# Selected and sliding attention heads wait for the copy of the compression's sums instead of the compressed keys

## The chip, the cores and the metric

The kernel runs on one core of one Trainium2 chip. The metric is the device time of one execution in microseconds (us); the median of the runs is compared. The engines are named as in the profile: PE (TensorE, matmuls), PEld (its weight loads), DVE (VectorE), ACT (ScalarE), POOL (GpSimd) and SP (SyncE, which issues most DMAs).

## The reference, cut to what matters

Two decoder layers on 256 rows of 1024 channels, all in float32. In each layer one projection of the normalised rows feeds three attentions, whose outputs are gated, lifted to 1024 channels, merged and projected again.

```python
def hybrid_layer(x, ...):
    h = rms_norm(x, norm_g)
    (mq, mk, mv, mz, nq, kc, vc, ksl, vsl, kw, vw, ng, nz,
     fq, fk, fv, ff, fz, gl) = split(h @ w_in)
    # A) MoBA, 6 heads: at 256 rows, plain causal attention with rope
    y_moba = (o_moba * silu(mz)) @ w_up_moba
    # B) NSA, 4 query heads over one key head, three branches:
    k_cmp = nsa_compress(kc, ...)      # blocks of 32 rows, every 16:
    v_cmp = nsa_compress(vc, ...)      #   silu((block + pe) @ w1) @ w2
    # o_c: softmax(q . k_cmp) v_cmp      compressed, 15 keys
    # o_s: softmax(q . ksl) vsl          selected (all 4 blocks, causal)
    # o_w: softmax(q . kw) vw            sliding (window 512, causal)
    o_nsa = gc[0] * o_c + gc[1] * o_s + gc[2] * o_w
    y_nsa = (o_nsa * silu(nz)) @ w_up_nsa
    # C) FoX, 6 heads: causal attention with a cumulated log forget gate
    y_fox = (o_fox * silu(fz)) @ w_up_fox
    merged = g[0] * y_moba + g[1] * y_nsa + g[2] * y_fox
    return x + merged @ w_out
```

Only o_c needs the compressed keys and values. o_s and o_w need q, ksl, vsl, kw, vw.

## The kernel before, in words

**Dense work.** Every weight is streamed from DRAM once, in tiles of up to 128 x 1024 values. For exactness each is split in two: ACT rounds the tile into its high part `wh` (L262), DVE subtracts that and keeps the remainder `wl` (L263). Each block of a product is then three matmuls (L287, L288, L289: `wh` with the high part of the activations, `wl` with it, `wh` with their remainder). They are called dense here; most have 384, 390 or 512 columns. Accumulators "acc" hold four banks of PSUM.

**Small work.** Heads and compression use PE between the dense matmuls. Tiles called "at" share a pool of three PSUM banks: which bank a new one takes is fixed when the kernel is built, and its first matmul waits until the last reader of the tile before it in that bank is done. They hold transposes of query and key columns (L475, for q: ACT copies half, L488, DVE takes the remainder, L489, and both again for the other half of the rows, twice for two tiles of rows), the sums' transpose and hidden layer of the compression (L804), the product with its second weight (L817), scores of a pair (L569, L582, L583, read by DVE's L589) and transposes of the exponentials (L596, read by L598 on ACT or L600 on DVE). One bank, "o", takes turns: first the sums U of the compression (L793, L794), then one group of head outputs after another (L604 to L608, L882).

**Compression.** `mm_w1` multiplies blocks by the first weight and leaves the sums U in bank "o". `cmp_post` copies them (L800), adds pairs of half blocks by a matmul (L804), applies the SiLU (L809 to L812), multiplies by the second weight (L817), normalises and rotates the key (L824 to L835), transposes it (L844) and lays it out for the four heads.

**What sets the order.** A planner lays out PE's whole list when the kernel is built. It holds a clock of planned time, which each dense step advances by 0.00042 us a column and matmul. `unit(generator, deps, lag)` puts a piece of small work on a list; it is due when its deps are done and the lag has passed, and each `yield` gives the planned time to its next part. `pairs` puts heads on the list two at a time. On PE this order is kept as written, so a small matmul that waits holds the dense ones behind it. The orders of DVE and ACT are made by a scheduler from the same program.

Dense blocks follow as in `run`: the NSA projections, `mq`, the first weight of the compression, `mz`, then `mk`, `fv`, `fq`, `fz`, `fk`, and the gate projections of 512 columns. `hs` are the selected and sliding heads, `hc` the compressed ones, `hm` MoBA's and `hf` FoX's; they take the bank "o" in this order of registration (`in_turn`).

Of the kernel before, what the change touches and what calls it, by code (L numbers as in the profile page):

```python
# [9 lines left out]
F32 = mybir.dt.float32  # L10
F32R = mybir.dt.float32r
AF = mybir.ActivationFunctionType
# [11 lines left out]
CL, CS, CH = 32, 16, 256  # L24
# [69 lines left out]
def trunk(ctx, tc, x, w_in, b_gate, cmp_w1, w_up_moba, w_up_nsa, w_up_fox, w_out, gains_d, eye_d, x_t, small_d, row_d, out):  # L94
    nc = tc.nc
    V, A, G, T = nc.vector, nc.scalar, nc.gpsimd, nc.tensor
# [90 lines left out]
    def unit(gen, deps=(), lag=1.5, limit=None):  # L187
        u = {"gen": gen, "deps": list(deps), "lag": lag, "limit": limit, "at": 0.0, "done": None}
        waiting.append(u)
        return u  # L190
# [159 lines left out]
    def layer(l):  # L350
        w = w_in[l]
        sh = {}
# [290 lines left out]
        def pairs(heads, deps):  # L643

            def both(hs):
                due = {}
                while len(due) < len(hs):
                    for i, h in enumerate(hs):
                        if i not in due:
                            lag = next(h)  # L650
                            if lag is not None:
                                due[i] = clock[0] + lag + i * SECOND
                while due:
                    i = min(due, key=due.get)
                    yield max(0.0, due[i] - clock[0])
                    try:
                        due[i] = clock[0] + next(hs[i])
                    except StopIteration:
                        del due[i]
            return [unit(both(heads[i:i + 2]), deps, LAG_K, HEADS) for i in range(0, len(heads), 2)]  # L660
# [33 lines left out]
        def nsa_heads(g):  # L694

            joints = [{} for _ in range(2)]

            def head(i, bank, rsum):
                h, b = 2 * g + i // 2, i % 2
                return attend(sh["nqs"][:, h, :], [sh[n][:, b, :] for n in ("kh2", "kl2")],  # L700
                              lambda kt: sh[("vsl", "vw")[b]][:, kt, :], i, bank, i, rsum, joint=joints[i // 2])
            return group(4, head, lambda bank, rsum: gated(bank, rsum, g))
# [81 lines left out]
        def mm_w1(b, ps):  # L784
# [3 lines left out]
            for q in range(8):  # L788
# [6 lines left out]
                if q % 4 == 3:  # L795
                    tick(8 * 0.11)

        def cmp_post():
            Us = wk.tile([64, CH], F32, name="zf", bufs=1)
            A.activation(Us[0:63], sh["U"][0:63, 0:CH], AF.Copy)  # L800
            yield 1.8
            ps = pat.tile([128, 512], F32, name="at")
            for c in range(2):
                T.matmul(ps[:, c * 32:c * 32 + 30], Us[0:63, c * 128:(c + 1) * 128],  # L804
                         tabs[0:63, K_SEL:K_SEL + 30], start=True, stop=True)
            hid = ps[:, 0:64].rearrange("p (c j) -> p c j", c=2)[:, :, 0:30]
            sg = sm.tile([128, 2, 30], F32, name="sg")
            hs = sm.tile([128, 2, 30], F32, name="hs")
            A.activation(sg, hid, AF.Exp, scale=-1.0)  # L809
            V.tensor_scalar(sg, sg, 1.0, None, op0=ALU.add)  # L810
            V.reciprocal(sg, sg)
            V.tensor_tensor(hs, hid, sg, op=ALU.mult)  # L812
            yield LAG_C
            ps = pat.tile([128, 512], F32, name="at")
            for kv in range(2):
                for c in range(2):
                    T.matmul(ps[0:NCMP, kv * HD:(kv + 1) * HD], hs[:, c, kv * NCMP:(kv + 1) * NCMP],  # L817
                             w2s[:, l, kv, c, :], start=c == 0, stop=c == 1)
            kc = sm.tile([16, 2, HD], F32, name="kc", bufs=1)[0:NCMP]
            vc = sm.tile([16, HD], F32, name="vc", bufs=1)[0:NCMP]  # L820
            ssc = sm.tile([16, 1], F32, name="ssc")[0:NCMP]
            rsc = sm.tile([16, 1], F32, name="rsc")[0:NCMP]
            jk = sm.tile([16, HD], F32, name="jk", bufs=1)[0:NCMP]
            A.activation(vc, ps[0:NCMP, HD:2 * HD], AF.Copy)  # L824
            A.activation(jk, ps[0:NCMP, 0:HD], AF.Square, accum_out=ssc)
            rsqrt(rsc, ssc, 1.0 / HD, (NCMP, 1))
            V.tensor_scalar(kc, ps[0:NCMP, 0:HD][:, None, :].to_broadcast([NCMP, 2, HD]), rsc, None, op0=ALU.mult)
            V.tensor_tensor(kc, kc, ncg[0:NCMP, l, :][:, None, :].to_broadcast([NCMP, 2, HD]), op=ALU.mult)
            ra = sm.tile([16, 2, 16], F32, name="ra")[0:NCMP]
            rb = sm.tile([16, 2, 16], F32, name="rb")[0:NCMP]  # L830
            cr = tabs[0:NCMP, K_CROPE:K_CROPE + 32]
            G.tensor_tensor(ra, kc[:, :, 0:16], cr[:, None, 0:16].to_broadcast([NCMP, 2, 16]), op=ALU.mult)
            G.tensor_tensor(rb[:, :, 0:8], kc[:, :, 8:16], cr[:, None, 16:24].to_broadcast([NCMP, 2, 8]), op=ALU.mult)
            G.tensor_tensor(rb[:, :, 8:16], kc[:, :, 0:8], cr[:, None, 24:32].to_broadcast([NCMP, 2, 8]), op=ALU.mult)
            G.tensor_tensor(kc[:, :, 0:16], ra, rb, op=ALU.add)  # L835
            kcb = lay.tile([128, 2, 32], F32, name="kcb")
            vcb = lay.tile([128, 4, HD], F32, name="vcb")
            G.memset(kcb, 0.0)
            G.memset(vcb, 0.0)
            for h in range(4):  # L840
                A.activation(vcb[32 * h:32 * h + NCMP, h, :], vc, AF.Copy)
            yield 7.0
            ps = pat.tile([128, 512], F32, name="at")
            T.transpose(ps[:, 0:NCMP], kc.rearrange("p a d -> p (a d)"), ident[0:NCMP, 0:NCMP])  # L844
            for a in range(2):
                V.tensor_copy(kcb[a * 64:a * 64 + 64, a, 0:NCMP], ps[a * 64:a * 64 + 64, 0:NCMP])
            sh["kcb"], sh["vcb"] = kcb, vcb
# [251 lines left out]
        def run(starts, following):  # L1099
            mm_first(starts)  # L1100
            if l == 0:
                mm("mv0")
                start_r()
                late_consts()
                rope_tables()
                ua = unit(post_a())
            else:
                start_r()
                rope_tables()
                ua = unit(post_a())  # L1110
                mm("mv0")
            cmp_zeros()
            uz = unit(cmp_tokens())
            mm("mv1")
            uv = unit(v_post("mv"))
            if l == 0:
                zero_lows()
                later_loads()
            mm("b0")
            finish(uz)  # L1120
            mm("w0")
            mm("b1")
            ub = unit(post_b())
            mm("mq0")
            mm("w1")
            mm("mq1")
            uq = unit(qk_post("mq"))
            mm("w2")
            mm("mz0")
            mm("mz1")  # L1130
            unit(z_post())
            mm("w3")
            uc = unit(cmp_post())
            hs = pairs(nsa_heads(0) + nsa_heads(1), [ua, ub, uc])
            hc = unit(cmp_heads(), [uc, ua], 1.5, HEADS)
            mm("mk0")
            mm("mk1")
            uk = unit(qk_post("mk"))
            hm = pairs(heads3("mq", "mk", "mv", 0, 0, False) + heads3("mq", "mk", "mv", 1, 0, False), [uq, uk, uv])
            mm("fv0")  # L1140
            mm("fv1")
            uv = unit(v_post("fv"))
            mm("fq0")
            mm("fq1")
            uq = unit(qk_post("fq"))
            mm("fz0")
            mm("fz1")
            uf = unit(fz_post())
            mm("fk0")
            mm("fk1")  # L1150
            uk = unit(qk_post("fk"))
            hf = pairs(heads3("fq", "fk", "fv", 0, 640, True) + heads3("fq", "fk", "fv", 1, 640, True),
                       [uq, uk, uv, uf])
            every = hs + [hc] + hm + hf
            for c in range(5):
                mm_gl(c, sh["gls"][c])
            finish(*every)
            g0, g1 = unit(gate_out(0)), unit(gate_out(1))
            unit(gate_sig(0))
            unit(gate_sig(1))  # L1160
            mm_gl(5, sh["gls"][5])
            unit(gate_sig(2))
            mm_up(0, sh["ups"][0], {0: [g0], 1: [g1]})
            m0 = unit(merged_T(0))
            mm_up(1, sh["ups"][1], {})
            m1 = unit(merged_T(1))
            finish(m0)
            state["sigs"] = sigs
            mm_out(sh["outs"], following)
            finish(m1)  # L1170
# [38 lines left out]
```

## Time and profile before

| what | value |
|---|---|
| median of 3 runs | 513.24 us (512.78 to 515.78) |
| profiled execution | 513.7 us, span 511.9 us |
| mean granted clock of PE | 0.997 |
| PE, PEld | busy 500.2 and 447.0 us |
| DVE, ACT, POOL | busy 399.9, 334.7 and 63.9 us |
| DMA | 92.31 MB, mean 180 GB/s |

The span runs from the first to the last instruction. A busy time is the time in which the engine had at least one instruction in flight; matmuls overlap, so the time from one start to the next is the price of a dense matmul, not its duration. A row of the timeline has the start, the duration, and in brackets the idle time before it with the instruction that ended it.

### The profile page before, as it was taken

The numbers are of one execution on the slowest core, as the hardware profiler recorded it, in microseconds if no ns is written. First come the engines' busy times: TensorE is split into PE (matmuls) and PEld (weight loads), VectorE is DVE, ScalarE is ACT, GpSimd is POOL, SyncE is SP. The second block draws the span as 40 slices with busy tenths as digits, with TensorE's granted clock in tenths as the row PEclk, the third lists the DMA queues.
The fourth block names the chain that finished last, engine by engine and source line by source line (L and its number), as shares of the span: only waits on it lengthen the run. The fifth ranks groups of instructions, "written<-read, shape, count | busy, mean of one in ns | idle before, by whom it ended". The sixth has DMA issues, their size and how long they took to land.

```text
span 511.9 us, 8226 instructions
## 1 busy us (share of the span) xinstructions
PE 500.2 (98%) x2806; PEld 447.0 (87%) x2806; DVE 399.9 (78%) x846; ACT 334.7 (65%) x645; POOL 63.9 (12%) x88
## 2 busy tenths in 40 slices
PE   9959999999999999999999999999999999999997
PEld 7859999999888888888889999999988888888886
DVE  6587988689986656998586998778997854698953
ACT  6677767877586675554376987678766866655440
POOL 3420121010020004024200000000101000142300
PEclk9998999999999999999999999999999999999999
DMA  8999885465665334655547699556547443537502
GB/s 288 323 224 239 218 270 162 131 217 165 190 203 183 121 93 160 193 178 180 170 124 189 185 242 278 184 154 194 180 157 242 144 148 101 165 125 229 178 5 82
DMA packets 58802, 92.31 MB, mean 180 GB/s; under 512 B 3964, under 2 KB 33288, under 8 KB 58760
## 3 DMA queue, kind: packets, MB, share of 16 engines
q1 hardware_dynamic: 56736, 89.67, 58.4%
q10 hardware_dynamic: 2024, 2.12, 1.3%
q8 instruction: 22, 0.36, 0.3%
q14 instruction: 20, 0.16, 0.1%
HBM read 90.71 MB, written 1.06 MB: 179 GB/s over the span
## 4 chain that ended last, share of the span: by engine, by line
PE 89%; ACT 5%; DVE 4%; issue 1%; ACTq 0%; DVEq 0%
PE acc L287 24%; PE acc L288 23%; PE acc L289 23%; PE at L596 2%; PE acc L1085 2%; ACT wh L262 2%; DVE wl L263 2%; PE at L582 1%; PE at L336 1%; PE at L583 1%; PE o L604 1%; PE o L608 1%; PE o L606 1%; PE o L794 1%; PE at L475 1%; PE o L793 1%
## 5 line engine op out<-in xcount | busy, mean ns | idle before, releaser
L263 DVE TENSOR_TENSOR wl<-st,wh 128x1024 fp32r<-128x1024 f32 (+4 forms) x180 | 200.6, 1122 | 51.3 <-ACT wh L262 49.8
L262 ACT ACTIVATE wh<-st 128x1024 fp32r<-128x1024 f32 (+4 forms) x180 | 170.6, 953 | 98.4 <-PE acc L289 71.9
L287 PE MATMUL acc<-wh,hT 128*128 128x512 f32 (+4 forms) x560 | 217.2, 388 | 1.8 <-ACT v L442 1.8
L288 PE MATMUL acc<-wl,hT 128*128 128x512 f32 (+4 forms) x560 | 203.0, 363 | 0.2 <-DVE wl L263 0.2
L289 PE MATMUL acc<-wh,lT 128*128 128x512 f32 (+4 forms) x560 | 203.2, 363 | 0.0
L289 PEld LDWEIGHTS acc<-wh,lT 128*128 128x128 f32 x560 | 105.4, 188 | 11.0
L287 PEld LDWEIGHTS acc<-wh,hT 128*128 128x128 f32 x560 | 106.1, 189 | 9.3 <-ACT v L442 2.1
L288 PEld LDWEIGHTS acc<-wl,hT 128*128 128x128 f32 x560 | 106.1, 190 | 7.2 <-DVE wl L263 0.7
L591 ACT ACTIVATE p<-p,nm 128x128 f32<-128x128 f32 x80 | 35.5, 445 | 17.4 <-DVE nm L589 17.2
L967 POOL TENSOR_TENSOR z<-z,tmp 128x512 f32<-128x512 f32 x8 | 12.9, 1649 | 108.3 <-ACT tmp L964 108.3
L287 PE MATMUL acc<-wh,qkT 128*128 128x512 f32 x64 | 25.6, 400 | 0.0
L289 PE MATMUL acc<-wh,qkT 128*128 128x512 f32 x64 | 25.0, 391 | 0.0
L288 PE MATMUL acc<-wl,qkT 128*128 128x512 f32 x64 | 25.0, 390 | 0.0
L1005 POOL TENSOR_TENSOR mg<-mg,tmp 128x512 f32<-128x512 f32 x8 | 15.8, 1996 | 51.5 <-DVE tmp L1004 51.5
L596 PE MATMUL at<-ident,p 128*128 128x128 f32 x120 | 19.8, 273 | 1.0 <-ACT qkT L496 1.0
L794 PE MATMUL o<-wl,Z 128*63 128x256 f32 x64 | 16.0, 287 | 3.3 <-DVE wl L263 3.3
L589 DVE CUSTOM_DVE_ANT_0 p<-at,tabs 128x128 f32<-128x128 f32 (+1 forms) x56 | 16.8, 349 | 2.7 <-ACT qkT L498 2.7
L953 DVE SCALAR_TENSOR_TENSOR gl<-acc,rt,tmp 128x512 f32<-128x512 f32 x24 | 17.0, 742 | 1.4 <-PE o L608 1.1
L596 PEld LDWEIGHTS at<-ident,p 128*128 128x128 f32 x120 | 15.0, 147 | 3.4 <-issue 1.6
L598 ACT ACTIVATE pt<-at 128x384 f32<-128x384 f32 x20 | 9.7, 487 | 9.8 <-PE at L596 9.4
L446 ACT ACTIVATE sq<-acc,rt 128x384 f32<-128x384 f32 (+2 forms) x28 | 13.7, 488 | 3.7 <-PE acc L289 3.2
L793 PE MATMUL o<-wh,Z 128*63 128x256 f32 x64 | 15.8, 285 | 0.1
(242 smaller groups left out, 685.6 us busy)
## 6 DMA issues: line engine op xcount, KB each, us to landing
st<-in_w_in_dram SPq DMA_DIRECT2D x52, 512.0 KB, 3.5
st<-in_w_in_dram SPq DMA_DIRECT2D x56, 384.0 KB, 4.3
st<-in_cmp_w_dram SPq DMA_DIRECT2D x32, 256.0 KB, 4.5
st<-in_w_out_dram SPq DMA_DIRECT2D x16, 512.0 KB, 4.3
st<-in_w_in_dram SPq DMA_DIRECT2D x8, 396.0 KB, 5.3
st<-in_w_in_dram SPq DMA_DIRECT2D x8, 390.0 KB, 3.1
tmp<-in_b_gate_dram SPq DMA_DIRECT2D x12, 256.0 KB, 3.7
st<-in_w_up_moba_dram SPq DMA_DIRECT2D x4, 512.0 KB, 3.6
```

Source lines behind the costliest of these rows:

```text
L262: return (lambda: A.activation(h, s_, AF.Copy), lambda: V.tensor_tensor(lo, s_, h.bitcast(F32), op=ALU.subtract))
L263: lambda: V.tensor_tensor(lo, s_, h.bitcast(F32), op=ALU.subtract))
L287: T.matmul(ps, sh, wh, start=first, stop=False)
L288: T.matmul(ps, sh, wl, start=False, stop=False)
L289: T.matmul(ps, sl, wh, start=False, stop=last)
L589: V.tensor_tensor_reduce(out=u, in0=sp, in1=add[t], scale=-SCALE, scalar=BIG, op0=ALU.add, op1=ALU.min, accum_out=nm)
L591: exps.append(A.activation(u, u, AF.Exp, bias=nm, scale=-1.0, accum_out=rsum[:, t, hb:hb + 1]))
L596: T.transpose(pts[:, s * 128:(s + 1) * 128], p[:, s * 128:(s + 1) * 128], ident)
L793: T.matmul(U, st, h, start=i == 0, stop=False)
L794: T.matmul(U, st, lo, start=False, stop=i == CL - 1)
L953: V.scalar_tensor_tensor(sh["gl"][t][b][:, n * 512:(n + 1) * 512], ps[t], sh["r"][:, t:t + 1], bg, op0=ALU.mult, op1=ALU.add)
L1005: (G if b == 1 else V).tensor_tensor(m, m, tmp, op=ALU.add)
```

## The change

The first step of `cmp_post`, the copy of U out of bank "o", becomes a unit of its own, `cmp_sums`. The rest of `cmp_post` is due 1.8 planned us after it, as before. The selected and sliding heads, which were registered to wait for the whole of `cmp_post`, wait for `cmp_sums`. The compressed heads wait for `cmp_post`, as before. All lines behind L802 move by 3, those behind L1133 by 4.

```diff
+        def cmp_sums():
+            sh["Us"] = wk.tile([64, CH], F32, name="zf", bufs=1)
+            A.activation(sh["Us"][0:63], sh["U"][0:63, 0:CH], AF.Copy)
+            yield 0
+
         def cmp_post():
-            Us = wk.tile([64, CH], F32, name="zf", bufs=1)
-            A.activation(Us[0:63], sh["U"][0:63, 0:CH], AF.Copy)
-            yield 1.8
+            Us = sh["Us"]
             ps = pat.tile([128, 512], F32, name="at")
...
-            uc = unit(cmp_post())
-            hs = pairs(nsa_heads(0) + nsa_heads(1), [ua, ub, uc])
+            us = unit(cmp_sums())
+            uc = unit(cmp_post(), [us], 1.8)
+            hs = pairs(nsa_heads(0) + nsa_heads(1), [ua, ub, us])
             hc = unit(cmp_heads(), [uc, ua], 1.5, HEADS)
```

Both lists of PE have 2425 rows with the same instructions. In the first layer the first score pair of the selected heads moves from row 412 to row 325, MoBA's first from 617 to 542, the last head product of the layer from 911 to 902; the transposes of the gated outputs (L336) stand in row 975 in both. The second layer shows the same pattern.

On PE, around the transposes of the first fq tile, the order before is this (buffer numbers stand behind the names; rows are left out where "..." stands).

```order
L475 MATMUL at_1534<-ident_94,qn_1318 128x128 [waits DVE_49]
L475 MATMUL at_1534<-ident_94,qn_1318 128x128 x2
...
L475 MATMUL at_1596<-ident_94,qn_1318 128x128 [waits Activation_49]
L475 MATMUL at_1596<-ident_94,qn_1318 128x128 x2
L608 MATMUL o_1581<-vsl_351,pt_1391 128x64
L596 MATMUL at_1605<-ident_94,p_1461 128x128 [waits DVE_49]
```

The bank of at_1534 is taken next by at_1605, 32 rows behind it, which waits for DVE's second L489 on at_1534. (The three tiles of transposes between them alternate in the other two banks.) In the new order, at the same place:

```order
L475 MATMUL at_1633<-ident_94,qn_1421 128x128 [waits DVE_49]
L475 MATMUL at_1633<-ident_94,qn_1421 128x128 x2
...
L885 MATMUL o_1656<-vcb_1049,pc_1612 128x256 [waits DVE_49]
L885 MATMUL o_1656<-vcb_1049,pc_1616 128x256 [waits DVE_49]
L596 MATMUL at_1667<-ident_94,p_1531 128x128 [waits Activation_49] x2
L596 MATMUL at_1667<-ident_94,p_1531 128x128
L582 MATMUL at_1674<-qkT_1091,qkT_737 128x128
L583 MATMUL at_1674<-klT_mk_102,qkT_737 128x128
L582 MATMUL at_1680<-qkT_1091,qkT_737 128x128 [waits DVE_49,PE_49]
```

Nine dense matmuls are left out. The second MoBA pair (at_1674, at_1680) has moved up behind the transposes, and at_1680 takes the bank of at_1633, 14 rows behind it; its wait on DVE is for the second L489 on at_1633.

On ACT the copies of the fq columns stood like this before:

```order
L591 ACTIVATE p,rsum<-p,nm 128x256
L488 ACTIVATE qkT<-at,tabs 64x3x128
L262 ACTIVATE wh<-st 128x1024
L488 ACTIVATE qkT<-at,tabs 64x3x128
L598 ACTIVATE pt<-at 128x384
```

And in the new order:

```order
L591 ACTIVATE p,rsum<-p,nm 128x256
L262 ACTIVATE wh<-st 128x768
L903 ACTIVATE e<-e 128x12
L442 ACTIVATE z_137<-acc,rt 128x384
L262 ACTIVATE wh<-st 128x1024
L488 ACTIVATE qkT<-at,tabs 64x3x128
L262 ACTIVATE wh<-st 128x1024
L488 ACTIVATE qkT<-at,tabs 64x3x128
L591 ACTIVATE p,rsum<-p,nm 128x128
```

The exponentials of a pair (L591) stand on both sides now; the split of 1024 columns between the two copies has stayed.

## Rows read from the trace of the kernel before

**Rows 1.** The page: busy time of the engines, and the chain by engine.

```profile
PE 500.2 (98%) x2806; PEld 447.0 (87%) x2806; DVE 399.9 (78%) x846; ACT 334.7 (65%) x645; POOL 63.9 (12%) x88
...
PE 89%; ACT 5%; DVE 4%; issue 1%; ACTq 0%; DVEq 0%
```

**Rows 2.** Waits of PE: total us, times, longest.

```profile
PE o L794 <- DVE wl L263: 3.3, 1, 3.3
PE acc L287 <- ACT v L442: 1.8, 1, 1.8
...
PE at L596 <- ACT qkT L496: 1.0, 2, 0.5
```

**Rows 3.** Timeline of PE: the two longest waits.

```profile
28.99 0.45 PE L287 MATMUL acc<-wh,hT 128*128 128x396 f32 x1 [1.82 <-ACT v L442]
...
37.93 0.47 PE L794 MATMUL o<-wl,Z 128*63 128x256 f32 x1 [3.28 <-DVE wl L263]
```

**Rows 4.** Windows: start:end, length, busy time by engine (x instructions), PE's granted clock, DMA.

```profile
26.00:37.60 11.60, 6.83 (x40) 6.20 (x39) 10.12 (x30) 9.45 (x17) 2.85 (x6) 1.00 1.00 238
37.60:41.00 3.40, 3.07 (x12) 3.08 (x13) 3.40 (x5) 0.84 (x1) 0.35 (x1) 0.50 0.46 123
...
74.00:100.00 26.00, 26.00 (x162) 25.27 (x160) 19.52 (x56) 19.55 (x48) 2.23 (x7) 1.00 0.55 163
100.00:140.00 40.00, 39.52 (x252) 36.61 (x251) 36.52 (x112) 27.86 (x63) 2.63 (x5) 1.00 0.60 190
```

**Rows 5.** Timeline of DVE: the last reader of the hidden sums.

```profile
75.86 0.22 DVE L812 TENSOR_TENSOR hs<-at,sg 128x60 f32<-128x60 f32 x1
```

**Rows 6.** Timeline of PE: a dense matmul in that stretch.

```profile
75.64 0.33 PE L287 MATMUL acc<-wh,hT 128*128 128x384 f32 x1
```

**Rows 7.** Timeline of PE: compressed heads' product, transposes and a MoBA pair.

```profile
140.27 1.02 PE L882 MATMUL o<-vcb,pc 128*128 128x256 f32 x4
141.13 0.49 PE L596 MATMUL at<-ident,p 128*128 128x128 f32 x3
141.37 0.30 PE L582 MATMUL at<-qkT 128*128 128x128 f32 x1
...
141.63 0.28 PE L582 MATMUL at<-qkT 128*128 128x128 f32 x1
```

**Rows 8.** Timeline of DVE: remainders of the fq columns and what stands between.

```profile
119.31 1.22 DVE L263 TENSOR_TENSOR wl<-st,wh 128x1024 fp32r<-128x1024 f32 x1
120.44 0.17 DVE L911 TENSOR_SCALAR y<-y 128x12 f32<-128x12 f32 x1
120.64 0.62 DVE L489 SCALAR_TENSOR_TENSOR qkT<-at,tabs,qkT 64x384 fp32r<-64x384 f32 x1
...
125.39 0.62 DVE L489 SCALAR_TENSOR_TENSOR qkT<-at,tabs,qkT 64x384 fp32r<-64x384 f32 x1
```

**Rows 9.** Timeline of PE: dense matmuls, both transposes of the fq columns.

```profile
115.54 0.33 PE L288 MATMUL acc<-wl,hT 128*128 128x384 f32 x1
...
115.89 0.49 PE L475 MATMUL at<-ident,qn 128*128 128x128 f32 x3
116.22 0.49 PE L596 MATMUL at<-ident,p 128*128 128x128 f32 x3
...
121.88 0.49 PE L475 MATMUL at<-ident,qn 128*128 128x128 f32 x3
...
122.38 0.50 PE L596 MATMUL at<-ident,p 128*128 128x128 f32 x3
```

**Rows 10.** Timeline of ACT: copies of the fq columns.

```profile
117.52 0.56 ACT L488 ACTIVATE qkT<-at,tabs 64x384 fp32r<-64x384 f32 x1
117.99 1.05 ACT L262 ACTIVATE wh<-st 128x1024 fp32r<-128x1024 f32 x1
119.06 0.58 ACT L488 ACTIVATE qkT<-at,tabs 64x384 fp32r<-64x384 f32 x1
```

**Rows 11.** Costliest groups by form, DVE, 74 to 136 us: count, busy, mean ns.

```profile
L589 DVE CUSTOM_DVE_ANT_0 p<-at,tabs 128x256 f32<-128x256 f32 x10 | 4.1, 414 | 0.0
```

## The prediction, made before the changed kernel ran

> **What bounds the kernel now.** I read the page first, then the waits of the matmul engine, then windows, then single stretches of the timeline. The page says that PE is busy 500.2 of 511.9 us, and that the chain that ended last is PE for 89% [rows 1]. The reader is to see that this is one engine working through one list: a change of order pays only where PE stood still. The table of PE's waits says where it did [rows 2]. The two largest, 3.3 and 1.8 us, lie at 37.9 and 29.0 us [rows 3], ahead of everything that this change moves. Behind that, the only wait of size is two times 0.5 us at L596, 1.0 us in all. All that is not busy is 511.9 - 500.2 = 11.7 us, so no order of the same work gains more than that, and the moved part can give back about 1 us.
>
> The windows then show what room the two helpers have [rows 4]. From 74 to 100 us PE is busy 26.00 of 26.00 us while DVE and ACT have 26.0 - 19.5 = 6.5 us free each. From 100 to 140 us DVE is busy 36.52 of 40.00. The first is where the selected and sliding heads go; in the second stretch they were, and MoBA's heads take their place there.
>
> **The change part by part.**
>
> *The split itself.* Same copy, same operations, the same 2425 rows on PE: nothing is added or removed, so 0 us of work.
>
> *The NSA heads start earlier.* Their first scores go from row 412 to row 325 of PE's order. In the planner they waited for a chain of 1.8 + 4.5 + 7.0 planned us, whose result they don't use. PE does the same matmuls between the same dense ones, so its sum stays (an operation set between two dense ones costs there what it cost before): 0. The end of a layer is not reached: the last head product goes from row 911 to 902, but the transposes of the gated outputs stand in row 975 in both. No gain there.
>
> *Score slots at the first NSA pair.* The second tile of the first pair takes the bank (slot, below) of the hidden sums and so waits for their last reader, L812, which ended at 75.86 + 0.22 = 76.08 [rows 5]. From the first column transposition of the mq columns (row 289 in both orders) the new one has 33 dense matmuls, the sums' L804 and a second column transposition ahead of this pair; the same stood ahead of the dense matmul that began at 75.64 [rows 6]. With the pair's first four score matmuls at 0.13 (two pairs of 0.26, [rows 7]) the slot is asked for at 75.64 + 0.52 = 76.16, just behind its reader. The helpers' order up to L812 is unchanged. I take 0.1 us, for a handshake that is not quite hidden; 0 below, 0.6 above, by half a remainder of a split (1.22, [rows 8]) that comes in its way. A second such place, a head's transposes behind the normalised compressed key, I put at 0 with the same bounds.
>
> *MoBA's second pair now stands right behind the fq columns.* This is the term. Before, the slot of the first fq tile (L475 at 115.89, [rows 9]) was asked for again at L596 (at_1605, row 578), seen at 122.38, 6.5 us later. The last reader, L489, was done at 120.64 + 0.62 = 121.26 [rows 8]: 5.37 us behind the transposes' start, and hidden. In the new order the same slot is asked for by the second score tile of a MoBA pair (at_1680, row 586, 14 rows behind). What lies between: the transposes 0.33 (115.89 to 116.22), nine dense matmuls at 0.175 = 1.57 (115.54 to 115.89 is two of them) [rows 9]; the four passes of the compressed heads' product 0.86 (140.27 to 141.13), a head's transposes 0.24 (141.13 to 141.37), one score pair 0.26 (141.37 to 141.63) [rows 7]. Sum 3.26 us. PE works in order, so what the columns take beyond that is lost by every dense matmul behind the score.
>
> How long will they take? ACT does copy, split of 1024 columns, copy [rows 10], and DVE the first remainder, the split's remainder, the second [rows 8], in the old order and the new. Link by link from those rows: 0.49 (transposes) + 0.56 + 1.05 + 1.22 + 0.17 (a small operation between) + 0.62 = 4.11 us; and the second fq tile took 125.39 + 0.62 - 121.88 = 4.13 [rows 8, 9]. The first took 5.37, because ACT was still in a pair's exponentials when the transposes ended and came to its copy at 117.52 [rows 10]. In the new order a MoBA pair's exponentials and the forget gate's small operations stand ahead of this tile as well, and it is the same tile, so 5.37 is the nearest row: 5.37 - 3.26 = 2.1 us of PE waiting. By the second tile's row it would be 0.9. The low end is 0: without the split between, copies and remainders are 0.49 + 2 x (0.56 + 0.62) = 2.85 us. The high end: DVE comes to it later by the four score passes of the MoBA pair, 4 x 0.41 = 1.6 us [rows 11], and 2.1 + 1.6 = 3.7.
>
> *The wait at L596 for the mk columns* (1.0 us in all, [rows 2]) stays in some form: 0, with 1.0 less or more as bounds.
>
> *Clock after the stall.* In the trace, the idle of 1.82 us before 28.99 was followed by a granted clock of 1.00 (the stretch from 26.0 to 37.6); that of 3.28 us before 37.93 by 0.50, the 1.2 GHz level, for 3.40 us, half of which, 1.7 us, is lost [rows 3, 4]. A stall of 2.1 us is nearer to the first: I count no loss, and keep the 1.7 as a bound. The Trainium skill ("TensorE: Matmul & The Clock Gate", section "What's actually happening") holds that the throttled state is the default and that activity releases it; by that rule alone each stall would be followed by a slow stretch, and the sum would be 3.4 us higher. The trace agrees for the 3.28 us idle and not for the 1.82 us one.
>
> *Second layer.* It is built by the same code and has the same places in the same order, so each term counts twice.
>
> **Sum.** 2 x (2.1 + 0.1) = 4.4 us. The profiled execution took 513.7 us (span 511.9 and 1.8 around it); with the change 518.1. The median of the three runs, 513.24, is 0.46 below it: 513.24 + 4.4 = 517.6 us, 0.9% slower.
>
> **The rivals.**
>
> *A: no stall, not slower.* The heads' scores, exponentials and copies move into 74 to 100 us, where DVE and ACT have 6.5 us free each, and leave the stretch where DVE had 3.5. Then ACT and DVE are ahead of PE at the fq columns, the columns take under 3.26 us, and the 1.0 us at L596 may go as well. Time: 513.24 - 1.0 = 512.2 to 513.2. For it: the free time; against it: a split of 1024 columns still stands between the two copies in either engine's order, and alone it makes 4.11. It decides below 3.3 us of column time. This is also the case in which the change does nothing at all: earlier heads bring no earlier end. Chance 0.22.
>
> *B: DVE becomes the bound.* MoBA's heads move into a stretch in which DVE has 3.5 us of 40 free [rows 4]. If it is late by the four score passes at the fq columns, 3.7, and by 0.6 at each of the two other slots, a layer loses 4.9 us: 513.24 + 9.8 = 523.0. For it: 91% busy DVE; against: the heads that leave take as much of it away. It decides once DVE is 1.6 us late there. Chance 0.14.
>
> *C: the clock falls.* The stall is long enough that the granted clock goes to 0.50 as at 37.93: 2 x (2.1 + 0.1 + 1.7) = 7.8, so 521.0. It decides somewhere between 1.82 and 3.28 us of idling [rows 3]. Chance 0.08.
>
> **How the numbers follow.** The forecast has 0.56, with its own range of 513.2 to 521 (0 to 3.7 per layer, and the 0.1). One per cent, about what a measurement of this kernel can tell from no change, is 5.1 us: 508.1 and 518.4. The forecast lies 0.8 us below the upper bound, so of its 0.56 I give 0.34 to the same and 0.22 to slower; B and C, 0.22, are slower; A gives 0.19 to the same and 0.03 to faster, for a gain that the waits shown do not contain. Together 0.03, 0.53, 0.44. The range runs from 512.5, which cuts off the lower part of A, to 522.5, which takes in C and cuts off most of B.
>
> **What would show it.** Right: a new row in PE's waits, a score matmul of L582 released by DVE's L489, once in each layer, some 2 us each; the first NSA scores some 15 us earlier (87 rows of about 0.175); the windows elsewhere as long as before; a granted clock of 1.00 around the stalls. Wrong: no such row (A); DVE without idle time and several waits of 0.5 us or more in the stretch (B); a window at 0.50 behind the stall (C); any shortening at a layer's end, which I exclude.

## The result, and the profile after

The changed kernel took 515.97 us (median of 19 runs, 514.54 to 518.28), the kernel before 513.58 us in 19 runs of the same sessions. The ratio is 1.0051, with a 95% interval of 1.0039 to 1.0063: slower by 2 to 3.2 us, less than one per cent. (Ratios and intervals are formed from all runs, and differ from the quotient of the two medians by up to 0.2%.) The forecast was 517.6 us, between 512.5 and 522.5, with the largest chance on less than one per cent and the next on slower.

The table of PE's waits of the changed kernel, in the columns of [rows 2]:

```profile
PE at L582 <- DVE qkT L489: 3.2, 2, 1.6
PE o L794 <- DVE wl L263: 3.1, 1, 3.1
PE acc L287 <- ACT v L442: 1.7, 1, 1.7
```

The first line is new, and it is the one that the prediction named: a score matmul of the second MoBA pair waits for DVE's remainder of the fq columns, once in each layer. The line of [rows 2] for L596, 1.0 us, is no longer among the larger ones: what is left of it is 0.11 us at 106.12 and 0.12 at 355.34. The two long waits at the start have stayed.

The timeline of PE around the new wait (compare [rows 7, 9]):

```profile
123.73 0.49 PE L475 MATMUL at<-ident,qn 128*128 128x128 f32 x3
...
125.64 1.03 PE L885 MATMUL o<-vcb,pc 128*128 128x256 f32 x4
126.50 0.49 PE L596 MATMUL at<-ident,p 128*128 128x128 f32 x3
126.75 0.31 PE L582 MATMUL at<-qkT 128*128 128x128 f32 x1
126.89 0.28 PE L583 MATMUL at<-klT_mk,qkT 128*128 128x128 f32 x1
128.77 0.30 PE L582 MATMUL at<-qkT 128*128 128x128 f32 x1 [1.60 <-DVE qkT L489]
```

From the transposes to the end of the first score pair (126.89 + 0.12, the next start without a wait) are 3.28 us; the prediction's sum was 3.26. From 126.89 to 128.77 are 1.88 us, where such a step takes 0.12 without a wait: the stop costs 1.76 us. The 1.60 in the brackets are counted from the end of the matmul before, and matmuls overlap, so a stop costs 0.16 us more than its idle time. What ACT and DVE do in that time (compare [rows 8, 10]):

```profile
123.20 1.05 ACT L262 ACTIVATE wh<-st 128x1024 fp32r<-128x1024 f32 x1
124.26 0.58 ACT L488 ACTIVATE qkT<-at,tabs 64x384 fp32r<-64x384 f32 x1
125.37 1.06 ACT L262 ACTIVATE wh<-st 128x1024 fp32r<-128x1024 f32 x1 [0.53 <-PE acc L289]
126.46 0.58 ACT L488 ACTIVATE qkT<-at,tabs 64x384 fp32r<-64x384 f32 x1
```

```profile
124.40 1.22 DVE L263 TENSOR_TENSOR wl<-st,wh 128x1024 fp32r<-128x1024 f32 x1
...
125.73 0.61 DVE L489 SCALAR_TENSOR_TENSOR qkT<-at,tabs,qkT 64x384 fp32r<-64x384 f32 x1
...
126.67 1.22 DVE L263 TENSOR_TENSOR wl<-st,wh 128x1024 fp32r<-128x1024 f32 x1
...
128.00 0.62 DVE L489 SCALAR_TENSOR_TENSOR qkT<-at,tabs,qkT 64x384 fp32r<-64x384 f32 x1
```

The columns are done at 128.62, 4.89 us behind the start of their transposes. The reader is to see two things. The second split of 1024 columns stands between ACT's two copies and itself stands still for 0.53 us, until PE frees a weight buffer. And DVE takes that split's remainder (126.67) ahead of the second L489.

The windows of [rows 4] again:

```profile
74.00:100.00 26.00, 26.00 (x174) 25.03 (x175) 21.52 (x67) 18.51 (x53) 2.40 (x8) 1.00 0.54 163
100.00:140.00 40.00, 38.29 (x248) 36.38 (x246) 33.67 (x105) 27.83 (x63) 3.54 (x8) 1.00 0.58 170
128.70:136.00 7.30, 7.23 (x47) 6.88 (x47) 5.92 (x27) 4.88 (x13) 1.43 (x2) 1.00 0.73 228
```

DVE went from 19.52 to 21.52 us in the first stretch and from 36.52 to 33.67 in the second; PE in the second from 39.52 to 38.29. (The changed kernel's profile is 1.9 us behind by then, so the stretches don't hold quite the same part of the program.) Behind the stall the granted clock is 1.00.

**The profiles differ by more than the medians**: the span is 516.5 against 511.9 us. A part of the difference, 1.9 of 4.6 us, lies ahead of all that the change moves. The first transposition of the mq columns is row 289 of PE's order in both kernels, with the same instructions ahead of it on every engine. In the kernel before, from there to PE's last matmul:

```profile
68.47 0.49 PE L475 MATMUL at<-ident,qn 128*128 128x128 f32 x3
...
508.50 0.28 PE L289 MATMUL at<-wh,lT 128*128 128x256 f32 x1
```

In the changed kernel:

```profile
70.36 0.49 PE L475 MATMUL at<-ident,qn 128*128 128x128 f32 x3
...
513.08 0.28 PE L289 MATMUL at<-wh,lT 128*128 128x256 f32 x1
```

From the first row's start to the last one's end (508.78 and 513.36) this rest is 440.3 and 443.0 us: 2.7 us longer, where the medians say 2.4; the other 1.9 us of PE's delay came before. Most of that is the clock's. In the kernel before it was at 0.50 until 41.0 [rows 4], in the changed one until 44.5 (13 matmuls where there were 21):

```profile
41.00:44.40 3.40, 3.40 (x21) 3.31 (x21) 1.18 (x2) 1.78 (x3) 0.00 (x0) 1.00 1.05 294
```

```profile
41.00:44.40 3.40, 3.40 (x13) 3.29 (x12) 0.97 (x2) 0.17 (x1) 0.00 (x0) 0.50 1.07 284
```

The start of row 289 differs by up to 3.6 us, 66.8 to 70.4, between the nine profiles below in which every engine has the same work in the same order up to it (in the three with both copies first, ACT and DVE have another order already at the start). So the rest is what is compared below, beside the medians: it follows the change, though from one profile each.

### The profile page after: what moved, and what is told of

Same layout as the page of the kernel before. It is cut to its first block, busy times and chain, and to the rows that moved or that the text cites. A ratio compares the mean times of both kernels' runs of the same rounds, so it can differ in the third digit from the quotient of the medians.

```text
span 516.5 us, 8219 instructions
## 1 busy us (share of the span) xinstructions
PE 502.1 (97%) x2806; PEld 448.4 (87%) x2806; DVE 402.4 (78%) x846; ACT 332.7 (64%) x645; POOL 62.8 (12%) x88
## 4 chain that ended last, share of the span: by engine, by line
PE 82%; DVE 7%; ACT 6%; DMA 3%; issue 1%; SPq 0%; ACTq 0%; DVEq 0%
PE acc L287 23%; PE acc L289 21%; PE acc L288 21%; DVE wl L263 3%; ACT wh L262 2%; PE at L596 2%; DMA st<-in_w_in_dram 2%; PE at L336 1%; PE at L582 1%; PE o L606 1%; PE o L604 1%; PE o L608 1%; PE o L794 1%; PE o L793 1%; PE at L583 1%
## 5 line engine op out<-in xcount | busy, mean ns | idle before, releaser
L591 ACT ACTIVATE p<-p,nm 128x128 f32<-128x128 f32 x80 | 35.4, 444 | 19.5 <-DVE nm L589 19.2
L596 PE MATMUL at<-ident,p 128*128 128x128 f32 x120 | 19.8, 274 | 0.2
L589 DVE CUSTOM_DVE_ANT_0 p<-at,tabs 128x128 f32<-128x128 f32 (+1 forms) x56 | 17.4, 351 | 0.9 <-PE at L583 0.7
L596 PEld LDWEIGHTS at<-ident,p 128*128 128x128 f32 x120 | 15.1, 147 | 2.8 <-ACT qkT L498 0.9
L582 PE MATMUL at<-qkT 128*128 128x128 f32 (+1 forms) x48 | 12.2, 289 | 3.2 <-DVE qkT L489 3.2
```

The costliest lines, as they stand in the source:

```text
L582: T.matmul(sp, q[:, qs], ks[0][:, 0:nk], start=True, stop=False)
L589: V.tensor_tensor_reduce(out=u, in0=sp, in1=add[t], scale=-SCALE, scalar=BIG, op0=ALU.add, op1=ALU.min, accum_out=nm)
L591: exps.append(A.activation(u, u, AF.Exp, bias=nm, scale=-1.0, accum_out=rsum[:, t, hb:hb + 1]))
L596: T.transpose(pts[:, s * 128:(s + 1) * 128], p[:, s * 128:(s + 1) * 128], ident)
```

## The experiments

The theory: the change costs two waits of 1.6 us at L582, gives back 0.73 of the 0.96 us at L596, and does nothing else. Its rivals: the time went somewhere else; or DVE is the bound in this stretch and a wait that is removed comes back beside it.

### The fq transposes behind the pair

```diff
-            yield LAG_Q
+            yield 12.5 if key == "fq" else LAG_Q
```

> The changed kernel, with a lag of 12.5 instead of 10 ahead of the transposes of the fq columns: they now stand behind the second MoBA pair, so no score matmul has to wait for their bank. Theory 1 (the change costs two waits of 1.6 us at L582 and gives back 0.75 us at L596): the L582 waits go, and 516.0 - 3.2 = 512.8 us, 0.1 to 0.2% under the kernel before. Theory 2 (the time went elsewhere, as in the first 56 us, where the changed kernel's profile is already 1.9 us behind): it stays at 515 to 516 us.

Measured: 513.98 us (before in these runs 512.97), ratio 1.001, interval 0.9994 to 1.0026. The waits at L582 went, and with them most of the loss. But it isn't below the kernel before, as theory 1 had it, since smaller waits came: L475 twice for DVE's copy L600 (0.26 and 0.66 us) and 0.32 us at L596.

### The fq transposes three matmuls later

```diff
-            yield LAG_Q
+            yield 10.75 if key == "fq" else LAG_Q
```

> The changed kernel with a lag of 10.75: the first fq transposes move three dense matmuls (0.52 us) closer to the score matmul that waits for them; the orders of ACT and DVE are unchanged. If the time of the columns counts from the transposes (the prediction's sum), each layer's wait grows by 0.5 to 2.1 us: 517.0 us. If it counts from the point where PE frees the weight buffer that ACT's split between the two copies waits for (125.37 in the changed kernel's trace), the last L489 ends when it did: wait 1.6 us each, 516.0 us.

Measured: 516.42 us, ratio 1.0053 (1.0036 to 1.0069). The waits are the same to 0.01 us. Of PE, ACT and DVE in the first layer:

```profile
123.30 0.49 PE L475 MATMUL at<-ident,qn 128*128 128x128 f32 x3
...
127.81 0.30 PE L582 MATMUL at<-qkT 128*128 128x128 f32 x1 [1.59 <-DVE qkT L489]
```

```profile
123.83 0.57 ACT L488 ACTIVATE qkT<-at,tabs 64x384 fp32r<-64x384 f32 x1 [0.54 <-PE at L475]
124.40 1.06 ACT L262 ACTIVATE wh<-st 128x1024 fp32r<-128x1024 f32 x1
```

```profile
125.70 1.22 DVE L263 TENSOR_TENSOR wl<-st,wh 128x1024 fp32r<-128x1024 f32 x1
...
127.04 0.62 DVE L489 SCALAR_TENSOR_TENSOR qkT<-at,tabs,qkT 64x384 fp32r<-64x384 f32 x1
```

The copy now waits 0.54 us for the transposes, and the split behind it no longer waits for its buffer: the slack of 0.53 us in the changed kernel's row is just used up. So the transposes do not set the end of the columns in the changed kernel; the split's buffer does, with copy, remainder and L489 behind it.

### The change in the first layer alone

```diff
-            hs = pairs(nsa_heads(0) + nsa_heads(1), [ua, ub, us])
+            hs = pairs(nsa_heads(0) + nsa_heads(1), [ua, ub, us if l == 0 else uc])
```

> The change in the first layer only; the second waits for the compressed keys as before. Theory 1: one wait of 1.6 us at L582, one of 0.5 us left at L596 of the second layer: half of the effect, 513.6 + 1.2 = 514.8 us. If one of the layers carries it all, 513.3 or 516.

Measured: 514.49 us, ratio 1.0026 (1.0011 to 1.004): half of the effect. One wait of 1.59 us at L582 is left. In the second layer the 0.5 us expected at L596 for the mk columns did not come. Another wait did, 42 us later in the layer: 0.72 us at L596 for DVE's L589, at 394.75.

### Both copies ahead of both remainders

```diff
             for r, o, d in halves(dst, t):
                 A.activation(d[r], p3[r], AF.Copy, scale=g[r])
+            for r, o, d in halves(dst, t):
                 V.scalar_tensor_tensor(d[o], p3[r], ...)
```

> The changed kernel with both of ACT's copies of a q tile written ahead of both of DVE's remainders; in ACT's order no split stands between the fq copies any more. If that split makes the wait: copies 124.26 to 125.4, remainders 125.73 to 127.0, asked for at 127.0, so 0 to 0.2 us of waiting in each layer and 516.0 - 3.0 = 513.0 us. If not the split but the work of DVE as a whole: wait 1 us or more, 515 us.

Measured: 514.08 us, ratio 1.0011 (0.9994 to 1.0029). Lines behind L488 are one higher here. In the first layer:

```profile
122.02 1.17 ACT L488 ACTIVATE qkT<-at,tabs 64x384 fp32r<-64x384 f32 x2
123.21 1.06 ACT L262 ACTIVATE wh<-st 128x1024 fp32r<-128x1024 f32 x1
```

```profile
125.11 0.30 PE L583 MATMUL at<-qkT 128*128 128x128 f32 x1 [0.19 <-DVE qkT L490]
```

The wait is 0.19 us where it was 1.60 (0.18 in the second layer). That split between the copies made it, with the same order on PE. But 0.31 and 0.74 us came at the next transposes, L597, for DVE's copy L601: the time is 1.1 us above the expected one.

### The fq transposes six matmuls earlier, and ten rows earlier

```diff
-            yield LAG_Q
+            yield 9.25 if key == "fq" else LAG_Q
```

(8.5 in the second kernel.)

> The changed kernel with a lag of 9.25: the first fq transposes stand six dense matmuls earlier, and with that both copies and remainders come ahead of the split whose weight buffer PE frees last. If the wait at L582 was that split's, it goes (0 to 0.2 us), and the other waits of the stretch (0.2 us in all) stay: 516.0 - 3.2 = 512.8, 0.1 to 0.2% under the kernel before. If DVE is the bound whatever the place, a wait of 0.5 us or more appears elsewhere, as 1.2 us did behind the pair: 514 us.

> The changed kernel with a lag of 8.5: the first fq transposes stand ten rows earlier, ahead of the compressed heads' transposes. By the waits of the stretch alone: no wait at L582, 512.8 us as for the lag of 9.25; a new wait can come at the compressed heads' product behind the moved columns, by 0.3 us each: 513.4 us.

Measured: 516.52 us, ratio 1.0062 (1.0041 to 1.0083), and 515.38 us, ratio 1.0047 (1.0028 to 1.0066), against 512.99 us. No idle time at L582 in either, and no gain. In the first of them:

```profile
126.62 0.28 PE L583 MATMUL at<-klT_mk,qkT 128*128 128x128 f32 x1
126.87 0.30 PE L582 MATMUL at<-qkT 128*128 128x128 f32 x1
...
129.61 0.55 PE L475 MATMUL at<-ident,qn 128*128 128x128 f32 x3 [0.23 <-DVE pt L600]
130.99 0.52 PE L596 MATMUL at<-ident,p 128*128 128x128 f32 x3 [0.83 <-DVE y L913]
```

```profile
126.84 1.22 DVE L263 TENSOR_TENSOR wl<-st,wh 128x1024 fp32r<-128x1024 f32 x1
...
128.18 0.43 DVE L688 TENSOR_TENSOR tmp<-o,wc 128x256 f32<-128x256 f32 x1
...
128.60 0.42 DVE L688 TENSOR_TENSOR tmp<-o,wc 128x256 f32<-128x256 f32 x1
...
129.00 0.55 DVE L600 COPY pt<-at 128x384 f32<-128x384 f32 x1
...
129.74 0.28 DVE L589 CUSTOM_DVE_ANT_0 p<-at,tabs 128x128 f32<-128x128 f32 x1
...
130.42 0.41 DVE L589 CUSTOM_DVE_ANT_0 p<-at,tabs 128x256 f32<-128x256 f32 x1
130.76 0.08 DVE L589 DVE_READ_ACCUMULATOR2_ANT nm<- 128x1 f32 x1
```

```profile
130.06 0.40 ACT L591 ACTIVATE p<-p,nm 128x128 f32<-128x128 f32 x1 [3.91 <-DVE nm L589]
...
131.41 0.49 ACT L591 ACTIVATE p<-p,nm 128x256 f32<-128x256 f32 x1
```

Here DVE runs from one instruction into the next, and ACT waits 3.91 us for it. PE computes the pair's scores from 126.47 to 127.8, and DVE comes to them at 129.74. The transposes at 130.99 belong to an earlier pair. They take the bank of this pair's first score tile and start behind DVE's second pass over it, done at 130.76 + 0.08 = 130.84; L913, which the row names, is only the operation that ran last. The pair's own exponentials can't be what they wait for: ACT's second one starts at 131.41. The waits of the stretch are 2.3 us in the first kernel and 2.4 in the second. In the second they did not come at the compressed heads' product, as expected, but at L475 (0.74 and 1.16 us) and L596 (0.31).

### Longer columns

```diff
-                V.scalar_tensor_tensor(d[o], p3[r], ...)
+                for _ in range((2 if l == 0 else 4) if key == "fq" and t == 0 and r.start else 1):
+                    V.scalar_tensor_tensor(d[o], p3[r], ...)
```

> The changed kernel, with DVE's second remainder of the first fq tile computed twice in the first layer and four times in the second (the same values again). If PE's wait at L582 follows the last remainder one to one, it grows in the first layer from 1.6 to some 2.9 us (one remainder of 0.62 and the 0.7 us that stand between in DVE's order) and in the second to over 4 us: 516.0 + 1.3 + 3 to 4 = 520 to 521.5 us. If the granted clock falls to 0.50 behind the longer waits, 1.7 us more for each: 522 to 525 us.

Measured: 524.15 us, ratio 1.0221 (1.0203 to 1.024). The waits are 3.00 and 5.07 us. The first ends behind the second remainder. The second does not end behind the fourth:

```profile
381.40 0.47 PE L583 MATMUL at<-qkT 128*128 128x128 f32 x1 [5.07 <-DVE pt L601]
```

```profile
380.79 0.56 DVE L601 COPY pt<-at 128x384 f32<-128x384 f32 x1
...
381.46 0.62 DVE L490 SCALAR_TENSOR_TENSOR qkT<-at,tabs,qkT 64x384 fp32r<-64x384 f32 x1
```

The matmul starts ahead of that remainder (381.46). In the second layer of this kernel its tile takes another bank, that of transposed exponentials, and waits for DVE's copy of them, L601, which stands behind three of the remainders. So the first wait alone follows the last remainder, as was expected; the second is another slot's, made longer by the same remainders. The windows behind each of them, in the columns of [rows 4]:

```profile
128.70:136.00 7.30, 7.29 (x47) 6.92 (x47) 5.72 (x25) 5.24 (x14) 1.08 (x2) 1.00 0.52 183
...
379.80:386.40 6.60, 5.00 (x19) 4.90 (x20) 4.42 (x23) 2.28 (x9) 0.72 (x1) 0.50 0.53 172
386.40:392.00 5.60, 5.60 (x35) 5.07 (x35) 4.17 (x5) 4.49 (x7) 0.00 (x0) 1.00 0.30 94
```

Behind 3.00 us of idling the granted clock is 1.00; within the 5.07 us it falls to 0.50, the 1.2 GHz level, and stays there until 386.4, five us behind the matmul at 381.40. A dense step takes 0.32 us there instead of 0.175, so some 2.3 of the five us are lost.

The length of a wait does not decide this. At the start of the kernel with the transposes ten rows earlier, the wait for L442 was 1.74 us, no longer than the 1.82 us of the kernel before [rows 3], behind which the clock was 1.00; yet it fell to 0.50 there until 32.4:

```profile
28.90 0.63 PE L287 MATMUL acc<-wh,hT 128*128 128x396 f32 x1 [1.74 <-ACT v L442]
```

```profile
28.90:32.40 3.50, 3.50 (x11) 3.50 (x12) 2.68 (x11) 3.12 (x7) 0.00 (x0) 0.52 1.06 331
```

The same came behind 1.73 and 1.74 us in both kernels with ACT's copies (below), and not behind 1.72 to 1.82 us in the eight others with a wait of that length at this place.

### MoBA's transposed exponentials copied by ACT

```diff
-            if h % 2:
+            if h % 2 or (joint is None and not bias):
                 A.activation(pt, pts[:, 0:384], AF.Copy)
             else:
                 V.tensor_copy(pt, pts[:, 0:384])
```

With both copies ahead of both remainders, and with the transposes behind the pair:

> The kernel with both copies ahead of both remainders, and with MoBA's transposed exponentials copied by ACT in every head, where DVE copied every second one. Of the waits that remained there, 0.31 and 0.74 us were for such a DVE copy. If DVE's queue was what made them: they go, 0.6 us of waiting is left in the stretch against 1.0 of the kernel before, and the time is 0 to 0.1% under it, 512.6 to 513.2 us. If ACT becomes late instead, waits for ACT's copies or for the split of weights appear, 514 us or more.

> The kernel with the fq transposes behind the second MoBA pair (lag 12.5), and MoBA's transposed exponentials copied by ACT in every head. There 0.26 and 0.66 us were waits of L475 for DVE's copy, 0.32 of L596. If DVE's queue made them they go: 513.0 us, even with the kernel before or 0.1% under. If a new wait for ACT replaces them: 514 us.

Measured: 512.17 us, ratio 0.9991 (0.9975 to 1.0006), and 514.41 us, ratio 1.0019 (1.0001 to 1.0036), against 513.5 us. In the first the waits for DVE's copy are gone, and no wait of the moved stretch is over 0.2 us:

```profile
PE at L583 <- DVE qkT L490: 0.3, 2, 0.2
PE at L583 <- ACT pt L599: 0.2, 1, 0.2
```

In the second 0.41 us for L589 and 0.25 and 0.16 us for ACT's copies took their place; 1.0 us of waiting in all, as in the kernel before, and the time is the 514 us that was expected if new waits came.

### A control: both copies first, without the change

The edit is the one on the copies, made in the kernel before.

> The kernel before with both of ACT's copies ahead of both of DVE's remainders, without the change: a control. If the order of the copies matters only where a score matmul waits for them, nothing changes here (513 us, waits of 1.0 us at L596). If it helps by itself, the gain of the copies-first kernel over the changed one (1.9 us) is partly seen here: 512 us or less.

Measured: 513.02 us, ratio 0.9987 (0.9971 to 1.0003); the two waits for the mk columns (L597 here) are there as before, 0.49 and 0.48 us, and no wait of the moved stretch has gone. In that stretch, what the order of the copies saves is the wait that the change made. Outside it, this order also removes the 0.36 us at L475 near 295 us, here and in the two other kernels that have it.

### All runs together

The rest is from the start of row 289 to the end of PE's last matmul in one profile; the waits are those over 0.1 us in it that the change or an edit can move (not the one at L475 near 295 us). The ratio's interval is from the timed runs.

| kernel | rest, us | over before | waits, us | over before | ratio, timed |
|---|---|---|---|---|---|
| before | 440.3 | | 1.0 | | |
| changed | 443.0 | 2.7 | 3.4 | 2.4 | 1.0039 to 1.0063 |
| fq behind pair | 441.2 | 0.9 | 1.5 | 0.5 | 0.9994 to 1.0026 |
| fq three later | 442.9 | 2.6 | 3.4 | 2.4 | 1.0036 to 1.0069 |
| first layer only | 442.0 | 1.7 | 2.4 | 1.4 | 1.0011 to 1.0040 |
| copies first | 441.0 | 0.7 | 1.7 | 0.7 | 0.9994 to 1.0029 |
| fq six earlier | 442.6 | 2.3 | 2.3 | 1.3 | 1.0041 to 1.0083 |
| fq ten earlier | 442.3 | 2.0 | 2.4 | 1.4 | 1.0028 to 1.0066 |
| longer columns | 450.1 | 9.8 | 8.3 | 7.3 | 1.0203 to 1.0240 |
| copies first, ACT copies | 440.2 | -0.1 | 0.8 | -0.2 | 0.9975 to 1.0006 |
| behind pair, ACT copies | 441.0 | 0.7 | 1.0 | 0.0 | 1.0001 to 1.0036 |
| before, copies first | 439.9 | -0.4 | 1.0 | 0.0 | 0.9971 to 1.0003 |

The two columns over before agree to within 0.7 us but for two rows. In six earlier, six stops stand against two, each 0.16 us dearer than its idle time, and the step to the second score tile takes 0.25 us (126.62 to 126.87) instead of 0.11 without any idle time shown, in both layers: 1.37 + 4 x 0.16 + 2 x 0.14 = 2.3 us, which is what the rest shows. In longer columns most of the 2.5 us between them are the clock's. In the three kernels with both copies first, some 0.5 us (0.36 + 0.16) of the gain in the rest is the wait near 295 us, which the change does not touch.

## Why the prediction was right, step by step

- **What bounds the kernel.** Right. PE went through the same instructions, and the rest of the span grew by its waits: 2.7 us for 2.4.
- **No gain from earlier heads.** Right: the selected heads' scores start at 77.53 us now, 7.2 us behind row 289 where it was 23.2 (91.67), and the end came no sooner. The stretch from 74 to 100 us took them in with PE busy 26.00 of 26.00.
- **The first NSA pair's slots.** Taken at 0.1 us a layer. In the first layer 0.1 came: the second tile's first matmul starts 0.23 us behind the one before it (77.89 and 78.12), where such a step takes 0.12. In the second layer the step took 0.12 (327.27 to 327.39), so nothing was lost.
- **The fq columns.** The place, the waiting instruction, the one waited for and the distance (3.26, measured 3.28) were right. The term was too large: columns of 5.37 us were taken from the first tile of the kernel before, 4.89 came, and the wait was 1.6 instead of 2.1 us (1.76 with the overlap that the stop costs). The reason given was wrong in part. In the changed kernel ACT was out of the exponentials at 122, and came to its first copy right behind the transposes. The time was set by the split between the copies, which waited for its buffer (three matmuls later: no difference; split taken from between: 0.19 us). The sum link by link, 4.11 us, had that split, but not the 0.53 us that it stands still nor the gaps on DVE. That 5.37 came nearer than 4.11, by way of a cause that wasn't there, is in part luck.
- **L596.** Put at 0 with a gain of 1.0 as bound; 0.73 us came back; no run was made on why. With the step before this makes the sum: 3.2 - 0.7 = 2.5 instead of 4.4 us.
- **The clock, and rival C.** None was lost: behind 1.6 us of idling the granted clock is 1.00. But the reason given, that a stall of 2.1 us lies nearer to 1.82 than to 3.28, is not borne out. 3.00 us in the middle of the layer left the clock at 1.00, where 3.28 us at the start [rows 3] were followed by 0.50, and so were 1.74 us at the start in another kernel; at 5.07 us it fell. The length of a wait alone does not tell the outcome between 1.7 and 3.3 us, so that no loss came is in part luck. The bound of 1.7 us was too high as well: of the 3.40 us at 0.50 PE worked in 3.1, from 37.93 to 41.0, and a dense step takes 0.33 us there (39.48 to 39.81) instead of 0.18, which makes 1.4. The Trainium skill's rule ("TensorE: Matmul & The Clock Gate", "What's actually happening"), that without activity the throttled state comes back, fits the 5.07 us.
- **Rival A** (no stall) did not come, but its second part did, the gain at L596. **Rival B** was not the case in the changed kernel, yet it is what the other orders ran into: each one that took the wait from L582 got 0.2 to 1.2 us at one or two of the next slots in each layer, where a bank was free only behind DVE, and they shrank to 0.4 us at most when ACT took over some of DVE's copies.

No version was clearly faster than both kernels. Copies first with ACT's copies is 0.6% under the changed kernel by the ratios, 0.1% of it by the wait near 295 us, and can't be told from the kernel before.

## What to carry to other kernels

Starting a piece of work earlier in an in-order queue pays nothing where that queue never stood still for it; what it moves together then decides. Before moving it, count for each shared buffer how much work lies between the step that fills it and its next writer, and compare that with what the readers' own queues have to do in between, splits that wait for buffers included. And where one engine behind has little room, expect a wait that was taken away in one place to come back a few slots on, until work is taken from that engine.

## What the hardware showed that was not expected

- The clock did not fall in 3.00 us of idling and did in 3.28 and 5.07, each in another place of the program; and at one and the same place it fell behind 1.74 us in some executions and did not behind 1.82 us in another.
- The same instructions at the start take 66.8 to 70.4 us from one profile to the next, more than the whole effect; a stretch with both ends behind it shows 0.5% in one profile.
